# Order and width of the products in the MLPs and the attention heads of a two-layer decoder trunk

## The chip, the cores and the metric

One core of a Trainium2 chip runs the whole program. The metric is the device time of one execution in microseconds (us). TensorE (PE) multiplies; its weight loads are a row of their own in the profile (PEld). VectorE (DVE) and ScalarE (ACT) do the elementwise work, GpSimd (POOL) very little, and SyncE (SP) issues nearly all transfers.

## The reference

The input is x, 256 tokens by 1024 features, in float32. There are two layers (DEPTH = 2). The first mixes tokens with a short gated convolution, the second with attention of 8 heads in 3 groups (each group has its own window and dilation). Each mixer is followed by a squared-ReLU MLP (1024 to 4096 and back to 1024) and a gated embedding:

```python
h = h + mixed
h = h + squared_relu_mlp(rmsnorm(h, norm_mlp[i]), mlp_w_up[i], mlp_w_down[i])
ple_gate = jax.nn.sigmoid(rmsnorm(h, norm_ple[i]) @ ple_w_gate[i])
h = h + ple_gate * (p[i].astype(h.dtype) @ ple_w_proj[i])
```

In the second layer the mixer computes q, k and v for 3 x 8 heads of 128 columns from the normalised h, rotates q and k, forms softmax scores in each group, weights the values with them and projects with w_o.

## The kernel before

**Two halves of a number.** Every weight and every activation is held as a high part (`whi`, `x[0]`) and a rest (`wlo`, `x[1]`), both in fp32r. A product of the two is whi*xhi + whi*xlo + wlo*xhi. Activations are kept transposed: features on the partitions, the 256 tokens along the free axis, high part and rest side by side (`x[2]`, 2 x 256 columns).

**Blocks.** `block` (L379) issues the products of one 128 x 128 block of weights (or of 384 or 512 columns of weights). There are three kinds:
- "w": the weights are stationary. One product of 256 columns (`wlo` on xhi) and one of 512 columns (`whi` on xhi and xlo at once) go into one PSUM bank of 512 columns. The two halves of the bank are added up later by ACT and DVE (`sums`, L419). This kind does the MLPs (`up0`, `down0`, `up1`, `down1`), q and k (`qkv`), most of the convolution's input and of the output projections. I call the two products of one block a pair.
- "n": three products of 256 columns.
- "t": activations stationary, weights moving, three products of 384 columns (v) or 512 columns (the last gate).

The order of the two products of a "w" block is set at L396: the second block of two (`half` = 1) has them reversed, so that the widths run 256, 512, 512, 256, 256, 512, 512, 256 ("paired" below). An exception is made for group 0 of heads 1 to 7: there no block is reversed, and the widths run 256, 512, 256, 512 ("alternating").

**The plan.** `make_plan` (L142) is a list of blocks and steps in program order. `mlp_plan` (L66) makes an MLP: `head_start` (L51) for the first two output column pairs, then 14 more, 8 blocks of k times 2 each, with a step `up_out` behind each; a small step `stat_rows` (L499, two products of 256 columns in a bank of their own, tile ssq) falls in the middle of the up part, behind its first 128 blocks. Then 4 x 32 x 2 blocks of the down part follow.

For head h the plan (L201 to L212) runs: q and k of group 0 (16 blocks); `scores(h-1)` (L683), which also issues the products of `values(h-2)` (L729); `add_up` of group 0, which empties its two PSUM banks; groups 1 and 2 with `qk_out` (rotation) between; `turn(h-1)` (L714: transposes of the softmax, tile tp, split into pT); then the head's values v (8 rows of 128 features, 2 blocks each, 3 products of 384 columns a block) with `qk_out` and `qk_split` between, and `v_out` (L664), which empties v's two banks. Head 1 is "late": `scores(0)` comes behind group 2 and `turn(0)` behind v.

**Weights.** They come from HBM in slabs in the order in which the plan first uses them (`make_slabs`, L248), of up to 8 blocks of 128 columns (512 KB), or two rows of v (384 KB). `split_to` (L358) splits a slab into whi (ACT, L368) and wlo (DVE, L307), five slabs ahead (`LOOK`), with 5 raw and 6 split buffers. PSUM has 8 banks under one tag. Each engine's order and all waits are made from this program order by the tile framework.

Of the kernel before, what the change touches and what calls it, by code (L numbers as in the profile page):

```python
# [18 lines left out]
NK = D // P  # L19
NP = NK // 2  # L20
FF = 4 * D
HEADS = 8
# [9 lines left out]
HURRY = 250  # L32
URGENT = ("gate_out", "mix_out", "down_out", "begin")
LOOK = 5
RAW_BUFS, SPLIT_BUFS, ACT_BUFS, PAIR_BUFS = 5, 6, 13, 20


# [104 lines left out]
def make_plan():  # L142
    plan = [("do", "begin")]
# [39 lines left out]
    def qk(h, g, ks):  # L183
        return [
            ("w", "qkv", k, (i, g, h), ("qk", h, g), i, "x3") for k in ks for i in (0, 1)
        ]

    def v(h, ks):
        return [("t", "v", k, h, ("v", b, h), b, "x3") for k in ks for b in (0, 1)]
# [10 lines left out]

    for h in range(1, HEADS):  # L201

        late, scores, turn = h == 1, [("do", "scores", h - 1)], [("do", "turn", h - 1)]
        for g in range(GROUPS):
            plan += qk(h, g, range(3)) + ([("do", "qk_out", h, g - 1)] if g else []) + qk(h, g, range(3, NK))
            if g == 0:
                plan += [("do", "qk_split", 0)] if late else scores
            elif g == 2:
                plan += scores if late else turn
            plan += [("do", "add_up", ("qk", h, g))]  # L210
        plan += v(h, range(2)) + [("do", "qk_out", h, 2)] + v(h, range(2, 4)) + [("do", "qk_split", h)]
        plan += v(h, range(4, NK)) + (turn if late else []) + [("do", "v_out", h)]  # L212

    last = HEADS - 1

# [50 lines left out]
def tile_trunk(ctx: ExitStack, tc: tile.TileContext, plan, slabs, ap, out):  # L266
# [17 lines left out]
    def pair(name, tag="pair", dtype=F32R):  # L284

        if tag == "pair":
            t = apool.tile([P, 2, 2, S], dtype, tag=tag, bufs=PAIR_BUFS, name=name)
        else:
            t = cpool.tile([P, 2, 2, S], dtype, tag=tag, bufs=1, name=name)
        return t[:, :, 0, :], t[:, :, 1, :], t  # L290
# [12 lines left out]
    def flat(t):  # L303
        return t.rearrange("p i s -> p (i s)")
# [12 lines left out]
    pos = const([P, S], "pos", I32)  # L317
    h = [held("h", f"h{j}", NP + 1) for j in range(NP)]
    state = {k: {} for k in ("u", "y", "p0", "p1", "qk", "pT", *(f"x{n}" for n in range(6)))}
    acc, left, opened = {}, {}, set()  # L320
    for op in plan:
        if op[0] != "do":
            key = ((*op[4], op[5]), 0) if op[0] == "w" else (op[4], op[5] if op[0] == "n" else 0)
# [7 lines left out]
    offsets, n = [], 0  # L331
# [47 lines left out]
    def block(kind, key, k, col, name, half, operand, m=0, cuts=1):  # L379
        name = (*name, half) if kind == "w" else name  # L380
        if name not in opened:
            acc[name] = bank("acc_" + "_".join(map(str, name)))
        left[name, half if kind == "n" else 0] -= 1
        whi, wlo = weights((key, k, col))
        x = state[operand][k // 2]
        if kind == "n":
            dst = acc[name][:, half, :]
            products = ((dst, wlo, x[0][:, k % 2, :]), (dst, whi, x[1][:, k % 2, :]), (dst, whi, x[0][:, k % 2, :]))

            products = (products[2], products[0], products[1]) if key == "proj0" else products  # L390
        elif kind == "w":

            dst = acc[name]
            products = ((dst[:, 0, :], wlo, x[0][:, k % 2, :]), (flat(dst), whi, flat(x[2][:, k % 2, :, :])))

            products = products[::-1] if half and (key != "qkv" or col[1] or not col[2]) else products  # L396
        else:
            n = width(key) * P // cuts
            whi, wlo = (t[:, m * n : (m + 1) * n] for t in (whi, wlo))
            dst = flat(acc[name])[:, :n]  # L400
            xhi, xlo = (t[:, k % 2, half * P : (half + 1) * P] for t in x[:2])
            products = ((dst, xhi, whi), (dst, xhi, wlo), (dst, xlo, whi))
        for n, (to, a, b) in enumerate(products):
            nc.tensor.matmul(  # L404
                to,
                a,
                b,
                start=n == 0 and name not in opened,
                stop=n == len(products) - 1 and left[name, half if kind == "n" else 0] == 0,
                skip_group_check=True,  # L410
            )
            opened.add(name)
# [269 lines left out]

    def scores(head):  # L683

        weights = cur["pr", head] = pair(f"sm{head}", dtype=F32)[2]
        ps = [psum.tile([P, 512], F32, tag="ps", name=f"sc{head}_{b}") for b in (0, 1)]
        rest = values(head - 1) if head else None
# [26 lines left out]
    def turn(head):  # L714


        sm = cur.pop(("pr", head))
        t = cur["pT12", head] = act(f"pT12_{head}")
        nc.vector.transpose(t[:, :, :P], sm[:, :, 1, :P])
        for q, k in ((0, 1), (1, 0), (0, 2), (1, 3), (2, 0), (3, 1), (2, 3), (3, 2)):  # L720
            rows, cols = (slice(n * 32, (n + 1) * 32) for n in (q, k))
            nc.vector.transpose(t[cols, :, rows], sm[rows, :, 1, cols])
        ps = bank(f"tp{head}")
        for b in (0, 1):
            for n in (0, 1):
                nc.tensor.transpose(ps[:, n, b * P : (b + 1) * P], sm[:, b, 0, n * P : (n + 1) * P], ident)
        split_into("pT", head, ps)
# [225 lines left out]
```

## Time and profile before

| | |
|---|---|
| median of 3 runs | 771.28 us (771.0 to 771.39) |
| profiled execution, its own time | 771.19 us |
| its span in the profile | 769.4 us |
| TensorE products | 4716 |
| PE, DVE, ACT busy | 761.2, 598.6, 488.7 us |

The span is what the profile's clock covers; the execution's own time has 1.8 us more around it. A product's row in the timeline gives its start and its length; products overlap, so the distance from one start to the next, not the length, is what a product costs the engine.

### The profile page before, as it was taken

What the parts mean: (1) busy time and instruction counts of PE and PEld (TensorE: products, weight loads), DVE (VectorE), ACT (ScalarE), POOL (GpSimd) and SP (SyncE); (2) the same over time, 40 slices, a digit from 0 to 9 for tenths busy, and PEclk for the clock granted to TensorE, in tenths of its full rate; (3) what the DMA queues carried; (4) which work ended last, traced back from release to release, by engine and by line L of the source; (5) the groups of instructions that cost most, each with busy time, mean ns of one, the idle gap of its engine ahead of it and who ended that gap; (6) DMA issues with size and microseconds to landing.
All of it is one profiled execution on the core that took longest, in us unless ns stands there. A gap on an engine that the chain in (4) does not pass through costs nothing.

```text
span 769.4 us, 12415 instructions
## 1 busy us (share of the span) xinstructions
PE 761.2 (99%) x4716; PEld 680.2 (88%) x4716; DVE 598.6 (78%) x967; ACT 488.7 (64%) x796; POOL 8.9 (1%) x22
## 2 busy tenths in 40 slices
PE   9999999999999999999999999999999999999996
PEld 9988888888888899989989989989988888888885
DVE  6898789898566668898988978977899887655564
ACT  7765566666444446688887778777666555444453
POOL 0000000000000000000000000000000000000002
PEclk9999999999999999999999999999999999999999
DMA  8855555556555554554555456456465555555521
GB/s 311 312 190 192 195 191 169 190 190 197 188 190 191 192 191 139 191 187 152 169 171 197 152 162 200 147 160 219 138 192 188 193 191 191 187 188 189 184 90 56
DMA packets 42539, 140.83 MB, mean 183 GB/s; under 512 B 4848, under 2 KB 6384, under 8 KB 42480
## 3 DMA queue, kind: packets, MB, share of 16 engines
q1 hardware_dynamic: 41904, 139.39, 54.3%
q8 instruction: 37, 0.61, 0.3%
q10 hardware_dynamic: 576, 0.66, 0.3%
q14 instruction: 22, 0.18, 0.1%
HBM read 138.97 MB, written 1.05 MB: 182 GB/s over the span
## 4 chain that ended last, share of the span: by engine, by line
PE 97%; issue 1%; DMA 1%; DVE 0%; POOL 0%; SPq 0%; POOLq 0%; ACT 0%; DVEq 0%
PE acc_u L404 23%; PE acc_d L404 23%; PE acc_qk L404 18%; PE acc_v L404 9%; PE acc_o L404 6%; PE acc_g L404 5%; PE acc_B L404 3%; PE acc_C L404 3%; PE acc_X L404 3%; PE acc_p L404 1%; PE o L736 1%; PE sc L692 1%; PE o L746 1%; DMA raw<-in_w 1%; PE sc L700 1%
## 5 line engine op out<-in xcount | busy, mean ns | idle before, releaser
L307 DVE TENSOR_TENSOR wlo<-raw,whi 128x1024 fp32r<-128x1024 f32 (+2 forms) x277 | 319.2, 1155 | 126.4 <-ACT whi L368 123.9
L368 ACT ACTIVATE whi<-raw 128x1024 fp32r<-128x1024 f32 (+2 forms) x277 | 277.9, 1007 | 166.2 <-PE acc_d L404 77.1
L404 PE MATMUL acc_u<-x,whi 128*128 128x512 f32 x512 | 160.8, 396 | 0.0
L404 PE MATMUL acc_d<-u,whi 128*128 128x512 f32 x512 | 160.8, 395 | 0.0
L404 PE MATMUL acc_qk<-x,whi 128*128 128x512 f32 x384 | 124.6, 395 | 0.0
L404 PEld LDWEIGHTS acc_d<-u,wlo 128*128 128x128 f32 x512 | 96.2, 188 | 22.7
L404 PEld LDWEIGHTS acc_u<-x,wlo 128*128 128x128 f32 x512 | 96.0, 188 | 22.5
L404 PE MATMUL acc_u<-x,wlo 128*128 128x256 f32 x512 | 101.3, 278 | 0.0
L404 PE MATMUL acc_d<-u,wlo 128*128 128x256 f32 x512 | 100.9, 278 | 0.0
L404 PE MATMUL acc_qk<-x,wlo 128*128 128x256 f32 x384 | 86.9, 280 | 0.0
L404 PEld LDWEIGHTS acc_qk<-x,wlo 128*128 128x128 f32 x384 | 72.1, 188 | 12.1
L404 PEld LDWEIGHTS acc_u<-x,whi 128*128 128x128 f32 x512 | 78.0, 189 | 0.2
L404 PEld LDWEIGHTS acc_d<-u,whi 128*128 128x128 f32 x512 | 77.9, 189 | 0.0
L404 PE MATMUL acc_v<-whi,x 128*128 128x384 f32 x256 | 67.2, 337 | 0.0
L404 PEld LDWEIGHTS acc_qk<-x,whi 128*128 128x128 f32 x384 | 62.5, 188 | 4.6
L404 PEld LDWEIGHTS acc_v<-whi,x 128*128 128x128 f32 x256 | 46.5, 188 | 0.1
L404 PE MATMUL acc_v<-wlo,x 128*128 128x384 f32 x128 | 42.9, 335 | 0.0
L423 ACT ACTIVATE r<-acc_u 128x256 f32<-128x256 f32 x64 | 24.1, 378 | 27.8 <-PE acc_u L404 27.5
L404 PE MATMUL acc_o<-y,whi 128*128 128x512 f32 (+1 forms) x144 | 41.0, 370 | 0.0
L655 ACT ACTIVATE rot<-qk 16x512 f32<-16x512 f32 x48 | 30.3, 632 | 9.9 <-DVE qk L424 9.2
L424 DVE TENSOR_TENSOR r<-acc_u,r 128x256 f32<-128x256 f32 x64 | 26.5, 419 | 3.5 <-ACT r L423 3.0
L404 PEld LDWEIGHTS acc_o<-y,wlo 128*128 128x128 f32 x128 | 24.0, 188 | 5.0
(175 smaller groups left out, 976.4 us busy)
## 6 DMA issues: line engine op xcount, KB each, us to landing
raw<-in_w SPq DMA_DIRECT2D x230, 512.0 KB, 3.6
raw<-in_w SPq DMA_DIRECT2D x32, 384.0 KB, 3.4
raw<-in_w SPq DMA_DIRECT2D x10, 256.0 KB, 4.9
h<-in_xT SPq DMA_DIRECT2D x4, 256.0 KB, 5.0
gain<-in_gain SPq DMA_DIRECT2D x2, 256.0 KB, 4.6
out<-htg SPq DMA_DIRECT2D x2, 256.0 KB, 2.1
mask<-in_mask SPq DMA_DIRECT2D x2, 192.0 KB, 3.4
raw<-in_w ACTq DMA_DIRECT2D x2, 128.0 KB, 3.7
```

Source lines behind the costliest of these rows:

```text
L307: nc.vector.tensor_tensor(out, a, f32(b), ALU.subtract)
L368: nc.scalar.activation(hi[:, :width], t[:, :width], AF.Copy)
L404: nc.tensor.matmul(to, a, b, start=n == 0 and name not in opened, stop=n == len(products) - 1 and left[name, half if kind == "n" else 0] == 0,
L423: nc.scalar.activation(t[:, i, :], p[:, 1, :], AF.Copy)
L424: nc.vector.tensor_tensor(t[:, i, :], p[:, 0, :], t[:, i, :], ALU.add)
L655: nc.scalar.activation(r[dst : dst + 16], p[src : src + 16], AF.Copy)
L692: nc.tensor.matmul(ps[b][:, :S], q[:, 0, own], k[:, 1, :], start=n == 0, stop=n == 2)
L700: nc.tensor.matmul(ps[b][r * 64 : (r + 1) * 64, at : at + 64], t[:, 0, of], t[:, 1, of], start=True, stop=True)
L736: nc.tensor.matmul(ps[:, 0, :], a, b[:, kb, :], start=kb == 0 and n == 0, stop=False, skip_group_check=True)
L746: nc.tensor.matmul(ps[to, 0, q], v12[:, b, r * P + m * 64 : r * P + (m + 1) * 64], t[:, b, r * 64 : (r + 1) * 64], start=False, stop=n == ...
```

## The change

An MLP's first six "w" blocks of the up part (k = 0 and 1 of the first two column pairs, as far as `LONG_AT[:6]` goes) get a wlo product of 384 columns instead of 256: it multiplies the first 128 columns of xlo too. Their order is 384, 512. All other blocks of the up and down parts are reversed, so that the widths alternate 512, 256. Elsewhere a "w" block is reversed always where the last blocks or steps before it were of kind "t" (the set `behind` holds "long"), and otherwise only in the second half, as before; a block of kind "n", `scores` and `turn` empty the set. The exception for group 0 is gone. For heads 2 to 6 two of the eight rows of v move from behind `turn` to behind `scores`, in front of group 1. In all heads `add_up` of a group now stands in front of `scores` or `turn`, not behind.

```diff
+LONG = {"up0": (6, 384), "up1": (6, 384)}
+LONG_AT = [(k, c + i) for c in (0, 2) for k in (0, 1) for i in (0, 1)]
...
+        rows = 0 if h in (1, HEADS - 1) else 2
         late, scores, turn = h == 1, [("do", "scores", h - 1)], [("do", "turn", h - 1)]
         for g in range(GROUPS):
             plan += qk(h, g, range(3)) + ([("do", "qk_out", h, g - 1)] if g else []) + qk(h, g, range(3, NK))
+            plan += [("do", "add_up", ("qk", h, g))]
             if g == 0:
-                plan += [("do", "qk_split", 0)] if late else scores
+                plan += [("do", "qk_split", 0)] if late else scores + v(h, range(rows))
             elif g == 2:
                 plan += scores if late else turn
-            plan += [("do", "add_up", ("qk", h, g))]
-        plan += v(h, range(2)) + [("do", "qk_out", h, 2)] + v(h, range(2, 4)) + [("do", "qk_split", h)]
-        plan += v(h, range(4, NK)) + (turn if late else []) + [("do", "v_out", h)]
+        plan += v(h, range(rows, 2 + rows // 2)) + [("do", "qk_out", h, 2)] + v(h, range(2 + rows // 2, 4 + rows // 2))
+        plan += [("do", "qk_split", h)] + v(h, range(4 + rows // 2, NK)) + (turn if late else []) + [("do", "v_out", h)]
...
+        if kind != "w":
+            behind.clear()
+            behind.update(("long",) if kind == "t" else ())
...
-            products = products[::-1] if half and (key != "qkv" or col[1] or not col[2]) else products
+            first = key in LONG and (k, col) in LONG_AT[: LONG[key][0]]
+            if first:
+                n = LONG[key][1]
+                products = ((flat(dst)[:, :n], wlo, flat(x[2][:, k % 2, :, :])[:, :n]), products[1])
+            elif key[:2] in ("up", "do") or "long" in behind:
+                products = products[::-1]
+            elif half:
+                products = products[::-1]
...
     def scores(head):
+        behind.clear()
...
     def turn(head):
+        behind.clear()
```

## Rows read from the trace of the kernel before

**Rows 1.** The page: busy time of the engines, and the granted TensorE clock in 40 slices (tenths of full speed).
```profile
PE 761.2 (99%) x4716; PEld 680.2 (88%) x4716; DVE 598.6 (78%) x967; ACT 488.7 (64%) x796; POOL 8.9 (1%) x22
...
PEclk9999999999999999999999999999999999999999
```

**Rows 2.** All that TensorE's two rows waited for, by the view of waits (engine, line, for whom: us in total, times, longest).
```profile
PE warm L531 <- DVE power L527: 1.0, 1, 1.0
...
PEld acc_p L404 <- DVE wlo L307: 0.3, 1, 0.3
```

**Rows 3.** The page's costliest groups, for the counts of products (busy us, mean ns of one, idle before).
```profile
L404 PE MATMUL acc_u<-x,whi 128*128 128x512 f32 x512 | 160.8, 396 | 0.0
L404 PE MATMUL acc_d<-u,whi 128*128 128x512 f32 x512 | 160.8, 395 | 0.0
```

**Rows 4.** Stretches (us from the span's start) with their length, PE's busy time and matmul records, granted clock, DMA share and GB/s: the first half of the up part in layer 0; its down part; group 0 of heads 3 and 4; groups 1 and 2 of head 4; the values of head 4. The records in brackets count neighbours that reach into the stretch.
```profile
101.92:146.51 44.59, 44.59 (x258) 1.00 0.61 199
191.34:280.51 89.17, 89.17 (x514) 1.00 0.55 189
385.65:391.20 5.55, 5.55 (x34) 1.00 0.71 217
413.84:419.39 5.55, 5.55 (x33) 1.00 0.71 227
421.98:433.25 11.27, 11.27 (x69) 1.00 0.41 138
433.60:442.03 8.43, 8.43 (x51) 1.00 0.52 178
```

**Rows 5.** PE's timeline (start us, length us, line, tiles, count): the first gate of layer 0, 60 products of 256 columns from the first row to the last.
```profile
280.51 0.28 PE L404 MATMUL acc_g<-x,wlo 128*128 128x256 f32 x1
...
287.71 0.51 PE L486 MATMUL ssq<-ones,tot 128*128 128x2 f32 x4
```

**Rows 6.** PE's timeline at the end: nine products of 512 columns of the last gate from the first row to the last.
```profile
751.86 0.39 PE L404 MATMUL acc_g<-whi,x 128*128 128x512 f32 x1
...
753.90 0.39 PE L404 MATMUL acc_p<-whi,p 128*128 128x512 f32 x1
```

**Rows 7.** PE's timeline at the start of group 0 of head 4: the first two pairs.
```profile
413.84 0.28 PE L404 MATMUL acc_qk<-x,wlo 128*128 128x256 f32 x1
413.96 0.40 PE L404 MATMUL acc_qk<-x,whi 128*128 128x512 f32 x1
414.19 0.28 PE L404 MATMUL acc_qk<-x,wlo 128*128 128x256 f32 x1
414.31 0.39 PE L404 MATMUL acc_qk<-x,whi 128*128 128x512 f32 x1
414.54 0.27 PE L404 MATMUL acc_qk<-x,wlo 128*128 128x256 f32 x1
```

**Rows 8.** PE's timeline at group 0 of head 2, right behind `turn(0)` (tile tp): its first pairs, and the first product behind its 16 pairs.
```profile
357.35 0.36 PE L404 MATMUL acc_qk<-x,wlo 128*128 128x256 f32 x1
357.55 0.40 PE L404 MATMUL acc_qk<-x,whi 128*128 128x512 f32 x1
357.79 0.28 PE L404 MATMUL acc_qk<-x,wlo 128*128 128x256 f32 x1
357.91 0.40 PE L404 MATMUL acc_qk<-x,whi 128*128 128x512 f32 x1
358.14 0.28 PE L404 MATMUL acc_qk<-x,wlo 128*128 128x256 f32 x1
...
363.00 0.87 PE L736 MATMUL o<-pT,v 128*128 128x256 f32 x6
```

**Rows 9.** PE's timeline, head 1: its 48 products of 384 columns of v behind `scores(0)`, from the first row to the last.
```profile
348.54 0.45 PE L404 MATMUL acc_v<-whi,x 128*128 128x384 f32 x1
...
357.00 0.60 PE L726 MATMUL tp<-ident,sm 128*128 128x128 f32 x4
```

**Rows 10.** PE's timeline at the start of the MLP of layer 1, and DVE's at the same time (the rests xlo of the MLP's first operand).
```profile
553.78 0.28 PE L404 MATMUL acc_u<-x,wlo 128*128 128x256 f32 x1
553.94 0.73 PE L404 MATMUL acc_u<-x,whi 128*128 128x512 f32 x2
554.51 0.40 PE L404 MATMUL acc_u<-x,wlo 128*128 128x256 f32 x2
...
553.40 0.88 DVE L448 SCALAR_TENSOR_TENSOR x<-hr,gains,x 128x256 fp32r<-128x256 f32 x2
```

**Rows 11.** DVE's timeline during head 4's blocks, behind `scores(3)`: the values' result, the second softmax pass, the emptying of group 0's banks; behind `turn(3)`: the split of pT and of head 4's qk.
```profile
422.35 0.42 DVE L758 TENSOR_TENSOR y<-o,y 128x256 fp32r<-128x256 f32 x1
422.69 0.55 DVE L707 CUSTOM_DVE_ANT_0 sm<-sc,mask 128x384 f32<-128x384 f32 x1
423.29 0.74 DVE L424 TENSOR_TENSOR qk<-acc_qk,qk 128x256 f32<-128x256 f32 x2
...
435.62 0.68 DVE L307 TENSOR_TENSOR pT<-tp,pT 128x512 fp32r<-128x512 f32 x1
...
436.88 0.68 DVE L307 TENSOR_TENSOR qk<-qk,qk 128x512 fp32r<-128x512 f32 x1
```

**Rows 12.** ACT's timeline behind the values of head 4: the copies of v for groups 1 and 2.
```profile
443.45 2.99 ACT L676 ACTIVATE v<-acc_v,n 64x128 f32<-64x128 f32 x8
```

**Rows 13.** PE's timeline behind group 0 of head 5: the products that read pT, qk and v.
```profile
447.58 0.87 PE L736 MATMUL o<-pT,v 128*128 128x256 f32 x6
448.29 0.88 PE L692 MATMUL sc<-qk 128*128 128x256 f32 x6
449.10 0.69 PE L746 MATMUL o<-pT,v 128*64 128x64 f32 x16
```

More of the change, by code (lines that the diff above doesn't have):

```diff
@@ L319, in tile_trunk @@
     state = {k: {} for k in ("u", "y", "p0", "p1", "qk", "pT", *(f"x{n}" for n in range(6)))}
-    acc, left, opened = {}, {}, set()
+    acc, left, opened, behind = {}, {}, set(), set()
     for op in plan:
```

## The prediction

> **What bounds the kernel now.** I read the page first: PE is busy 99% of the span, PEld 88%, DVE 78%, ACT 64%, and the granted clock is in the top tenth in every slice [rows 1]; the stretches show 1.00 of full speed, the 2.4 GHz level [rows 4]. Then the waits: both TensorE rows together waited 1.3 us, all of it at the start [rows 2]. So no transfer, split or bank holds PE up, and the time is the sum over 4716 products of what each costs from its start to the next start. A change helps only if it lowers that sum, and hurts as soon as it adds columns or a wait.
>
> So I measure what a product costs in each order of widths. Uniform widths first: 60 products of 256 columns take 287.71 - 280.51 = 7.20 us, 120.0 ns each [rows 5]; nine of 512 take 753.90 - 751.86 = 2.04 us, 226.7 ns each [rows 6]. At 2.4 GHz 256 and 512 columns alone are 106.7 and 213.3 ns, so every product pays 13.3 ns on top, and a pair without loss is 346.7 ns. The MLPs run paired: the down part of layer 0 has 256 pairs (512 in both layers [rows 3]) in 89.17 us, 348.3 ns a pair, and the first 128 pairs of its up part take 44.59 us, again 348.3 [rows 4]. The alternating order stands in the trace too, in group 0: 16 pairs in 5.55 us in heads 3 and 4, 346.9 ns with the first pairs in it [rows 4]. Those first two pairs take 414.54 - 413.84 = 0.70 us [rows 7], which leaves 4.85 us for the other 14, 346.4 ns, which is 346.7 within the rows' rounding. Head 2 enters the same order from transposes and not from wide products: after its first pair it needs 363.00 - 357.79 = 5.21 us for 15 pairs, 347.3, and 346.8 without the second pair (358.14 - 357.79 = 0.35) [rows 8]. So alternating products cost 1.7 ns a pair less than paired ones.
>
> **The change part by part.**
>
> *Order in the MLPs.* There are 1024 pairs; 12 become long, 1012 go from 348.3 to 346.7: 1012 x 1.66 = 1.68 us less. From the row with its entry pairs in it (346.9) it would be 1.45 us. I take the lower price, since 500 pairs in a row are nearest to the settled ones.
>
> *The long products.* 2 x 6 blocks have 384 + 512 columns. A product of 384 costs 13.3 + 160 = 173.3 ns with the same 13.3; v's 48 take 8.43 us, 175.6 with their entry [rows 4]. A long pair is 226.7 + 173.3 = 400 ns, 51.7 over a paired one: 12 x 51.7 = 0.62 us more.
>
> *Order in the heads.* Groups 1 and 2 of heads 2 to 6 become alternating, 5 x 32 pairs x 1.66 = 0.27 us less. In head 1 the same holds for 32 pairs (no `scores` comes between), and for the first 20 pairs of w_o behind head 7's v: 0.09 less. Group 0 of head 2 stands behind `turn(0)` and goes back to paired: 0.03 more. Sum: 0.33 less.
>
> *Two rows of v behind the scores.* No product is added. What moves is the break that PE has behind the small products of `scores`. Now group 1 pays it: groups 1 and 2 of head 4 take 11.27 us, 0.12 over 32 x 348.3 ns [rows 4]. With v behind `scores`, v pays it: head 1 shows that, 357.00 - 348.54 = 8.46 us for 48 products, 0.14 over 48 x 173.3 [rows 9]. Five times 0.02 is 0.10 us more. v's break behind `turn` stays.
>
> *Start of layer 1's MLP.* The first three products, of 256, 512 and 512 columns, take 554.51 - 553.78 = 0.73 us, 0.16 over their 0.57, because the second reads xlo, whose first of two DVE pieces ends about 553.84, half of its row [rows 10]. A product of 384 columns reads xlo already, so the wait falls before the first product, with a weight load behind it: start about 554.05 in place of 553.78, 0.27 lost in place of 0.16 (an estimate from the piece's end and the 0.12 to 0.14 us that PE lost at the breaks above). I take 0.11 us more; bounds are 0.16 less (xlo earlier) and 0.3 more.
>
> *At nothing:* `add_up` in front of `scores` puts 0.74 us of DVE [rows 11] and two ACT passes ahead of the softmax; `turn` comes 11.3 us later now and 13.4 us later then. Moving a quarter of v's 8.43 us takes 2.1 us from the stretch between `turn` and the next `values`. pT is split by 436.3 and qk by 437.6, wanted at 447.58 and 448.29 [rows 11, 13]: 11 and 10 us of slack become 9 and 8. v's copies end at 446.44, wanted at 449.10 [rows 12, 13]; their distance from v's last product does not change, but up to 2.1 us more ACT work lies near it, against 2.7 us of slack. v holds two PSUM banks during groups 1 and 2; the banks of `o`, `sc` and group 0 are empty by 422.8, 423.3 and 424.0, 2.1 us at most behind the end of `scores` (421.98), and the moved v rows last 2.1 us, so group 1 finds banks. The slab of the moved rows is one of the same four of v; number and order kind stay, so SP's queue gets no more issues. If that cover fails, a head loses between nothing and the 2.1 us by which its stretch is shorter; I keep 1 us in each of 5 heads as the bound, since ACT is idle 36% of the time.
>
> **Sum:** -1.68 + 0.62 - 0.33 + 0.10 + 0.11 = -1.18 us. From the profiled execution's 771.19 that is 770.0; the median is 0.09 higher, so 770.1. About 0.2% (1.54 us) is what a measurement of this kernel can tell from no change; the forecast lies inside.
>
> **The rivals.**
>
> 1. *The order is worth nothing in the MLPs*: the 1.7 ns come from something else there than order. Then only the added columns are left: 771.28 + 0.62 + 0.10 + 0.11 = 772.1 at most. Against it: paired pairs cost 348.3 in the up part, reading x, and in the down part, reading u [rows 4]. Chance 0.11. The Trainium skill, page "TensorE: Matmul & The Clock Gate", section "Back-to-back issue gap", would have it so: it gives an isolated warm gap of N/2.4 + 2.5 ns, whatever product stands before, and by it the change would only add 12 x 128 columns, an estimate of 0.64 us from that page. The trace disagrees with it in the size, 13.3 ns and not 2.5 [rows 5, 6], and in that order matters [rows 4].
>
> 2. *Slower: the alternation settles in a worse cycle.* In the up part two products of 256 (`stat_rows`) come behind 128 blocks, in both layers; no wide product follows them, and nothing restores what the long ones set up. The entry pairs show that alternation can cost more: 0.35 us each [rows 7, 8], up to 355 ns with the rows' rounding. If it stays at 351, a little over the rows, for the 384 pairs behind that point, 768 x 2.7 = 2.1 us are added and their 1.27 us of gain are lost: 771.28 - 1.18 + 1.27 + 2.1 = 773.5. It decides from 350.2 ns a pair on (where the sum passes +1.54). Against it: head 2 left that cost after two pairs without wide products [rows 8], and no alternating stretch of the trace keeps it. Chance 0.13.
>
> 3. *A wait in the heads* takes the place of the reordering's gain: v's copies or the softmax come late by up to 1 us in five heads, giving 770.1 to 775.1, 772.6 in the middle. Slack of 2.7 us at the narrowest speaks against it [rows 12, 13]. Chance 0.08.
>
> 4. *More than forecast:* layer 1's wait vanishes, the breaks cost less: -1.68 - 0.33 + 0.62 - 0.15 = -1.54, 769.7, at the bound of what can be told. Chance 0.13.
>
> **How the numbers follow.** Forecast 0.55, and rival 1, 0.11, lie within 0.2%; so do the cheap ends of 2 and 3, 0.04 of their 0.21; 0.01 of the forecast reaches beyond 1.54. Same 0.69; slower 0.17; faster 0.13 + 0.01 = 0.14. The range takes in rivals 4 and 1 and the cheaper half of 3, and leaves out rival 2 and the rest, under 0.2: 769.5 to 772.9.
>
> **What would show it.** Right: in the profile after, the down part takes 256 x 346.7 = 88.75 us instead of 89.17, the part of the up part behind `stat_rows` 44.4 instead of 44.6, and its first part 44.7, where the long products give back the gain; groups 1 and 2 together 11.1 us behind v, without a break in front; no PE wait in the heads. Wrong: a down part of 89.2 or more, alternate pairs at 350 or more behind ssq, or PE waits on ACT at `values`.

## The result, and the profile after

The changed kernel takes 774.02 us (median of 5 runs, 773.71 to 774.38) against 771.24 for the kernel before on the same chip: ratio 1.0036, 95% interval [1.0025, 1.0048]. It is slower by 2.8 us, where the forecast was 770.1 and the range ended at 772.9. The clock is the same, so the place has to be found in stretches.

The page after, answering to [rows 1]: the same number of products, PE busy 2.3 us longer. Nothing in this view tells why.
```profile
PE 763.5 (99%) x4716; PEld 682.1 (88%) x4716; DVE 598.4 (77%) x967; ACT 484.1 (63%) x796; POOL 8.9 (1%) x22
...
PEclk9999999999999999999999999999999999999999
```

Stretches of the kernel after, as in [rows 4] (start and end, length, PE's busy time and records, clock, DMA share, GB/s): layer 0's up part before and behind its `stat_rows`, its down part; the same three of layer 1; groups 1 and 2 of head 4; from the start of w_o to the MLP of layer 1.
```profile
101.86:147.41 45.55, 45.55 (x258) 1.00 0.57 195
147.64:192.87 45.23, 45.23 (x258) 1.00 0.57 187
192.87:283.32 90.45, 90.45 (x514) 1.00 0.54 186
557.06:602.05 44.99, 44.99 (x256) 1.00 0.57 186
602.29:646.67 44.38, 44.38 (x259) 1.00 0.57 190
646.67:735.41 88.74, 88.74 (x514) 1.00 0.57 190
426.80:437.90 11.10, 11.10 (x66) 1.00 0.52 174
529.00:557.06 28.06, 27.54 (x215) 1.00 0.58 193
```
The same change of order cost 1.28 us in layer 0's down part (90.45 against 89.17) and saved 0.43 in layer 1's (88.74). In pairs: 90.45 / 256 = 353.3 ns and 88.74 / 256 = 346.7. Paired blocks took 348.3. Added up against the kernel before: layer 0's up part with `stat_rows` +1.60, its down part +1.28, layer 1's up part +0.01, its down part -0.43, the heads -0.43 (221.75 against 222.18), w_o +0.90, the start -0.06: +2.87, which is the 2.8 us of the spans (772.2 against 769.4) within rounding.

What 353.3 looks like, in PE's timeline of the kernel after in layer 0 (start, length; the distance from start to start is the price):
```profile
104.65 0.40 PE L420 MATMUL acc_u<-x,whi 128*128 128x512 f32 x1
104.89 0.28 PE L420 MATMUL acc_u<-x,wlo 128*128 128x256 f32 x1
105.01 0.40 PE L420 MATMUL acc_u<-x,whi 128*128 128x512 f32 x1
105.24 0.28 PE L420 MATMUL acc_u<-x,wlo 128*128 128x256 f32 x1
105.36 0.40 PE L420 MATMUL acc_u<-x,whi 128*128 128x512 f32 x1
105.59 0.28 PE L420 MATMUL acc_u<-x,wlo 128*128 128x256 f32 x1
105.71 0.40 PE L420 MATMUL acc_u<-x,whi 128*128 128x512 f32 x1
```
Three pairs take 105.71 - 104.65 = 1.06 us, 20 ns over three times 346.7, with no wait in any row. The trace's starts in full ns give the pairs (512, then 256) as 232/118, 241/120, 236/114, and so on without end. I call this **the costly cycle**. There are two **cheap cycles**, both of 346.7 ns a pair: an even one, every pair 230/117, and one of two pairs, 233/117 and 231/113. Group 0 of heads 3 to 7 has the two-pair cycle in the kernel before and the even one in the kernel after. In layer 1 of the kernel after the costly cycle ends without any added break, here:
```profile
568.63 0.40 PE L420 MATMUL acc_u<-x,whi 128*128 128x512 f32 x1
568.87 0.40 PE L420 MATMUL acc_u<-x,wlo 128*128 128x256 f32 x2
569.11 0.40 PE L420 MATMUL acc_u<-x,whi 128*128 128x512 f32 x1
569.35 0.28 PE L420 MATMUL acc_u<-x,wlo 128*128 128x256 f32 x1
569.47 0.39 PE L420 MATMUL acc_u<-x,whi 128*128 128x512 f32 x1
569.70 0.27 PE L420 MATMUL acc_u<-x,wlo 128*128 128x256 f32 x1
569.81 0.40 PE L420 MATMUL acc_u<-x,whi 128*128 128x512 f32 x1
```
Two products of 256 stand side by side at 568.87 (x2), as two of 512 do earlier, at 560.29, where one 512 was issued ahead of its turn; from 569.35 on a pair takes 0.34 to 0.35 us.

w_o's 0.90 us is another matter. About 0.7 of it is a wait of TensorE for pT, and 0.24 is the entry into the MLP behind it (more on both below). The view of waits, answering to [rows 2]; the 1.0 us at the start is there as before, and new is:
```profile
PEld o L754 <- DVE pT L311: 0.7, 1, 0.7
PE o L754 <- DVE pT L311: 0.4, 1, 0.4
```
DVE's timeline after, before the last head's values (wlo splits, first softmax pass, split of pT), and PE's row that waits:
```profile
537.37 2.36 DVE L311 TENSOR_TENSOR wlo<-raw,whi 128x1024 fp32r<-128x1024 f32 x2 [2.77 <-ACT whi L372]
539.64 0.55 DVE L724 CUSTOM_DVE_ANT_0 sm<-sc,mask 128x384 f32<-128x384 f32 x1
...
548.83 0.68 DVE L311 TENSOR_TENSOR pT<-tp,pT 128x512 fp32r<-128x512 f32 x1
```
```profile
549.57 0.62 PE L754 MATMUL o<-pT,v 128*128 128x256 f32 x3 [0.45 <-DVE pT L311]
```
The kernel before, at the same place, of which the prediction has no row: DVE's split of pT, and PE's first product that reads it. It ends at 546.48 and is read from 546.60, so there was 0.1 us of slack and not the 11 of head 4 [rows 11, 13].
```profile
545.80 0.68 DVE L307 TENSOR_TENSOR pT<-tp,pT 128x512 fp32r<-128x512 f32 x1
```
```profile
546.60 0.57 PE L736 MATMUL o<-pT,v 128*128 128x256 f32 x3
```

### The profile page after: what moved, and what is told of

It is laid out like the page before. It is cut to its first block, busy times and chain, and to the rows that moved or that the text cites. A ratio compares the mean times of both kernels' runs of the same rounds, so it can differ in the third digit from the quotient of the medians.

```text
span 772.2 us, 12419 instructions
## 1 busy us (share of the span) xinstructions
PE 763.5 (99%) x4716; PEld 682.1 (88%) x4716; DVE 598.4 (77%) x967; ACT 484.1 (63%) x796; POOL 8.9 (1%) x22
## 4 chain that ended last, share of the span: by engine, by line
PE 95%; DVE 1%; issue 1%; ACT 1%; DMA 1%; POOL 0%; SPq 0%; POOLq 0%; DVEq 0%
PE acc_u L420 23%; PE acc_d L420 23%; PE acc_qk L420 17%; PE acc_v L420 9%; PE acc_g L420 5%; PE acc_o L420 4%; PE acc_B L420 3%; PE acc_C L420 3%; PE acc_X L420 3%; PE acc_p L420 1%; DVE wlo L311 1%; PE o L754 1%; PE sc L709 1%; PE o L764 1%; DMA raw<-in_w 1%
## 5 line engine op out<-in xcount | busy, mean ns | idle before, releaser
L420 PE MATMUL acc_u<-x,whi 128*128 128x512 f32 x512 | 179.7, 396 | 0.0
L420 PE MATMUL acc_d<-u,whi 128*128 128x512 f32 x512 | 179.3, 396 | 0.0
L420 PE MATMUL acc_u<-x,wlo 128*128 128x256 f32 (+1 forms) x512 | 143.6, 281 | 0.1
L420 PE MATMUL acc_d<-u,wlo 128*128 128x256 f32 x512 | 142.8, 279 | 0.0
L420 PE MATMUL acc_qk<-x,whi 128*128 128x512 f32 x384 | 130.5, 392 | 0.0
L420 PEld LDWEIGHTS acc_d<-u,whi 128*128 128x128 f32 x512 | 96.1, 188 | 23.1
L420 PEld LDWEIGHTS acc_u<-x,whi 128*128 128x128 f32 x512 | 96.0, 188 | 22.9
L420 PE MATMUL acc_qk<-x,wlo 128*128 128x256 f32 x384 | 100.5, 280 | 0.0
L420 PEld LDWEIGHTS acc_qk<-x,whi 128*128 128x128 f32 x384 | 68.5, 187 | 11.4
L671 ACT ACTIVATE rot<-qk 16x512 f32<-16x512 f32 x48 | 30.3, 632 | 29.5 <-DVE qk L440 28.9
L692 ACT ACTIVATE v<-acc_v,n 64x128 f32<-64x128 f32 x64 | 23.2, 363 | 12.7 <-DVE v L688 11.9
```

The lines of the kernel that those rows point to most:

```text
L420: nc.tensor.matmul(to, a, b, start=n == 0 and name not in opened, stop=n == len(products) - 1 and left[name, half if kind == "n" else 0] == 0,
L671: nc.scalar.activation(r[dst : dst + 16], p[src : src + 16], AF.Copy)
L692: nc.scalar.activation(v12[to, b, r * P : (r + 1) * P], p[own, g * P : (g + 1) * P], AF.Copy, scale=scale[own])
```

## The experiments

Two questions: what turns the alternation costly, and what made w_o wait. The expectations give theories letters: **A**, how TensorE comes into a stretch (out of a running stream or from a break); **B**, the place (layer 0, but not layer 1); **C**, the long products; **D**, which width comes first; **P** and **F**, the place in the cycle at which the order of widths breaks; **U**, a run of one width. Layer 0 and layer 1 are L0 and L1, kernel n is that of experiment n, ssq the two products of `stat_rows`. Lengths are from PE's timeline; a half of the up part has 128 pairs, so 45.2 is the costly cycle, 44.4 a cheap one and 44.6 the paired order; for a down part 90.45, 88.75, 89.17.

**1. A break of the order in layer 0.** The changed kernel, but L0's blocks run 256 first from k = 4 on.
```diff
+            elif key in ("up0", "down0") and ("flip" in opened or (key, k, col) == ("up0", 4, 0)):
+                opened.add("flip")
             elif key[:2] in ("up", "do") or "long" in behind:
                 products = products[::-1]
```


> The changed kernel, and in layer 0 the order turns once: from the block k = 4 of the first column on, up0 and down0 run 256, 512 in place of 512, 256, so two products of 256 columns stand side by side once, as they do by chance in layer 1 at 569 us. Theory A (the order has two steady cycles, 346.7 and 353.3 ns a pair, and what stands directly before decides which one it runs in; two 256s side by side lead out of the slow one): layer 0 runs at 346.7 from there on, some 490 pairs x 6.67 ns = 3.3 us less than the changed kernel, 774.0 to 770.8. Rival B (layer 0 is slow because of what lies in layer 0: its operands, buffers, the other engines' work): it stays at 353.3, down part 90.4 us, 774.0. Rival D (256 first is the fast order, 512 first the slow one): layer 0 gets fast too, but then layer 1, 512 first and fast, is not explained.

771.59 us, ratio 1.0004 [0.9994, 1.0013]. The two 256s side by side, behind a pair 232/118, did not lead out: the half is costly. But at ssq, where three 256s stand together, L0 turned cheap: 44.37 and 88.75. So the costly cycle is no property of L0 or of its operands, and a broken order can end it, though not everywhere.

**2 and 3. Each order alone, no long products, heads as before.**
```diff
-... if half and (key != "qkv" or col[1] or not col[2]) else products
+... if half and key[:2] not in ("up", "do") and (key != "qkv" or col[1] or not col[2]) else products
```
```diff
+... if key[:2] in ("up", "do") or half and (key != "qkv" or col[1] or not col[2]) else products
```


> The kernel before, with the MLPs alone alternating, 256 first, no long products, heads as before. Layer 0 is entered from paired products that end in 256, so that two 256s stand side by side at the entry. Theory A: 346.7 ns a pair from the start in layer 0, without any long product: down part 88.75 us, 1.7 us less in both MLPs if layer 1 does the same: 769.6. Rival B: layer 0 at 353.3, down part 90.4 us: 771.3 + 2.6 - 0.9 = 773.0. Rival C (the long products are what makes the fast cycle, and were only too few): both layers at 353.3, 776.4.

> The kernel before, with the MLPs alone alternating, 512 first, no long products, heads as before. Layer 0 is entered without two 256s side by side. Theory A: layer 0 at 353.3 ns a pair (+2.6 us against paired), as with the long products, so that these do nothing; layer 1 falls to 346.7 if the scheduler again sets two 256s side by side (-0.85 us), else where its entry puts it: 773.0 or 776.4. Rival B: the same in layer 0. Rival C: both layers at 353.3, 776.4. Together with the 256-first kernel it tells A from B: the two differ in layer 0's first products alone.

256 first: 773.08, 1.0024 [1.0014, 1.0034]; L0 costly throughout (45.22, 45.23, 90.46), L1 is cheap behind its first 33 blocks (44.57, 44.38, 88.75). Those blocks hold some costly pairs too, up to 567.6 us, where two products of 512 stand side by side. 512 first: 775.74, 1.0059 [1.0043, 1.0075]; L0 costly, L1 cheap up to ssq (44.46) and costly behind it (45.23, 90.45). C falls: no long product is needed. D falls: both orders have both cycles.

**4. The heads alone**: the changed kernel with the MLPs paired.
```diff
-LONG = {"up0": (6, 384), "up1": (6, 384)}
+LONG = {}
-            elif key[:2] in ("up", "do") or "long" in behind:
+            elif key[:2] not in ("up", "do") and "long" in behind:
```


> The changed kernel's heads alone: MLPs paired as before, no long products. From the two traces: q, k and v of the heads 0.43 us less, the projection behind them 0.90 us more, since the values of the last head wait for the split of pT. Theory: 771.3 - 0.4 + 0.9 = 771.8, down parts at 89.17 us as before. Rival (the wait in the projection comes from the changed MLPs' load on DVE and ACT, not from the heads): 770.8.

771.52, 1.0004 [0.9995, 1.0014]. The MLPs are back at 89.17, the heads keep their 0.43 us gain, and w_o keeps its wait (`o` for pT, 0.5 us in the PE row; w_o takes 27.85 us against 27.17 before). The two leave +0.26 us in the span (769.65 against 769.39).

**5. Each half entered from a drained TensorE**: kernel 3 with one small float32 product in front of each up part and behind each ssq.
```diff
+    def drain():
+        keep(nc.tensor.matmul(bank("drain")[:, 0, :2], ones, ones[:, :2], start=True, stop=True))
```


> The kernel before with the MLPs alone alternating, 512 first, no long products (as the earlier kernel that had layer 0 at 353.3 ns a pair), and one added fp32 product of ones on two columns of ones, in a bank of its own that nothing reads, ahead of each up part and behind the two products of stat_rows: four in all. In the traces the fp32r product behind such a product starts 0.08 us late, with PE emptied. Theory A2 (the alternation runs at 346.7 when PE enters it emptied, and falls to 353.3 when it is entered from running paired products or thrown out of step by others): both layers at 346.7 throughout, down parts 88.75 us, 1.7 us less, four breaks of about 0.25 us more: 770.6. Rival B (layer 0 is slow for what lies in it): layer 0's down part stays at 90.4: 771.3 + 2.6 - 0.9 + 1.0 = 774.0. Rival P (pure chance of phase, no rule by entry): some of the four stretches fast, some slow.

776.38, 1.0066 [1.0054, 1.0079]. Only L1's first half is cheap (44.47); L0 on both sides of ssq (45.31, 45.31) and L1 behind ssq (45.31) are costly, though each was entered behind a break (the 512 behind it takes 323 or 324 ns to the next start instead of some 230). A falls.

**6. Long products of 512**, so that twelve products of one width open each MLP.
```diff
-LONG = {"up0": (6, 384), "up1": (6, 384)}
+LONG = {"up0": (6, 512), "up1": (6, 512)}
```


> The changed kernel with long products of 512 in place of 384 columns, so that an MLP begins with twelve products of one width, 512. Theory A2: PE is not emptied by that, layer 0 stays at 353.3 ns a pair: 774.0 + 0.6 = 774.6. Rival U (a run of one width sets the fast cycle, as the values' 384s do in the heads; the 384 beside 512 failed because they alternate themselves): layer 0 at 346.7, its down part 88.75 us: 774.6 - 3.4 = 771.2.

772.95, 1.0021 [1.0012, 1.003], neither of the two times foretold. The uniform run leads into the costly cycle in both layers (45.84 and 45.93, the added columns in them); at ssq, coming behind a pair of 232 to 233 and 118 to 119 ns, both turn to the even cheap cycle (44.38, 88.75). ssq behind 241/125, in the kernel after and in kernel 3, did not do that.

**7. Alternation everywhere**, on top of kernel 5.
```diff
-... if key[:2] in ("up", "do") or half and (key != "qkv" or col[1] or not col[2]) else products
+            products = products[::-1]
```


> As the kernel with the four added fp32 products, and every block of stationary weights in the kernel is reversed (512, 256), in the convolution, the projections and all groups of q and k too; no block or step is moved. Theory A2: groups 1 and 2 behind scores, where PE is emptied by small products, run at 346.7 without two rows of values moved there (11.20 us in place of 11.26); the convolution behind its fp32 products as well; stretches entered from running products of 256 (the projection behind the convolution, head 0) may go either way. About 500 more pairs, 0.8 us less if all are fast: 769.8; 2.5 us more if those 500 are slow: 773.1.

777.95, 1.0087 [1.0074, 1.0101], far above the 773.1 foretold as the worst: both halves of L0 and L1 behind ssq are costly as in kernel 5. Groups 1 and 2, each time behind the same small products and the same break, take 11.20 us in heads 2, 4 and 6 and 11.40 in heads 3, 5 and 7; group 0 behind v (heads 3 to 7) is cheap every time (5.55). Heads 4 and 5, stretches as in [rows 4]:
```profile
426.14:437.34 11.20, 11.20 (x68) 1.00 0.46 146
454.28:465.68 11.40, 11.40 (x68) 1.00 0.45 142
```
So a short break does not reset what decides: starts that agree within 2 ns (the first 512 takes 335 or 334) go on in the two-pair cycle in one head and in the costly one in the next.

**8. An early turn**: kernel 2, but the first two blocks of L0 have 512 first, so the order turns behind the second pair of the cycle.
```diff
+            if key[:2] in ("up", "do"):
+                products = products[::-1] if key == "up0" and (k, col) in [(0, 0), (0, 1)] else products
+            elif half and (key != "qkv" or col[1] or not col[2]):
+                products = products[::-1]
```


> The kernel before, MLPs alternating, no long products, heads as before. In layer 0 the first two blocks run 512, 256 and all later ones 256, 512, so that two 256s stand side by side once, behind the second pair; layer 1 runs 256, 512. In the earlier runs the slow cycle repeats every three pairs, with starts 232/118, 241/120, 235/114 ns apart, and two 256s led out of it behind the second of these (twice of two, layer 1) and not behind the first (once of one, layer 0). Theory F (the cycle is a matter of phase: the same products at the same point of the cycle end the same way): layer 0 runs at 346.7 ns a pair from the third block to stat_rows; what the three 256s there do depends on the phase too and is open: 346.7 behind them gives 771.3 - 0.85 - 0.67 (layer 1 as measured with 256 first) = 769.8, 353.3 gives 772.3. Rival A2 (entered from running paired products it stays slow): 353.3 throughout layer 0, 773.1.

772.13, 1.0009 [1.0, 1.0018]. PE's timeline at the turn:
```profile
102.29 0.40 PE L409 MATMUL acc_u<-x,whi 128*128 128x512 f32 x1
102.53 0.40 PE L409 MATMUL acc_u<-x,wlo 128*128 128x256 f32 x2
102.77 0.40 PE L409 MATMUL acc_u<-x,whi 128*128 128x512 f32 x1
103.00 0.28 PE L409 MATMUL acc_u<-x,wlo 128*128 128x256 f32 x1
103.12 0.39 PE L409 MATMUL acc_u<-x,whi 128*128 128x512 f32 x1
103.35 0.27 PE L409 MATMUL acc_u<-x,wlo 128*128 128x256 f32 x1
```
Behind the two 256s at 102.53 a pair takes 0.35 us, up to ssq: L0's first half 44.40, where kernel 2, without the turn, has 45.22. Theory F foretold this from the place where L1 of the kernel after left the costly cycle, also behind 241/120. Behind ssq L0 is costly again (45.23, 90.46).

**9. The sums back in their old place**: kernel 4 with `add_up` behind `scores` and `turn`.
```diff
-            plan += [("do", "add_up", ("qk", h, g))]
...
+            plan += [("do", "add_up", ("qk", h, g))]
```


> The changed kernel's heads without the moved add_up (it stands behind scores and turn again), MLPs paired as before, no long products. Theory: the 0.7 to 0.9 us that the projection behind the heads lost come from the moved add_up, which makes ACT wait for DVE in the rotation (28.9 us in the page of the changed kernel) and lets DVE split pT of the last head late; without it the values of the last head do not wait, and the heads' alternation stays: 771.3 - 0.4 = 770.9. Rival (the moved rows of v make DVE late): 771.5 as with the heads alone.

770.83, 0.9993 [0.9984, 1.0002], 0.69 us below kernel 4, the only difference being `add_up`; in the traces w_o takes 27.13 us against 27.85, and the heads are the same. DVE's timeline at the end of the heads:
```profile
531.54 2.48 DVE L311 TENSOR_TENSOR wlo<-raw,whi 128x1024 fp32r<-128x1024 f32 x2 [2.75 <-ACT whi L372]
535.43 0.56 DVE L724 CUSTOM_DVE_ANT_0 sm<-sc,mask 128x384 f32<-128x384 f32 x1 [1.41 <-PE sc L717]
...
545.17 0.68 DVE L311 TENSOR_TENSOR pT<-tp,pT 128x512 fp32r<-128x512 f32 x1
```
Here DVE waits 1.41 us for the scores before the softmax; in the kernel after the two wlo splits were only done at 539.64 and the softmax had to wait for them. PE has no wait for pT any more.

**10. A run of 384 columns in front of each half**: kernel 3 with 48 added products.
```diff
+    def run_in():
+        to = flat(bank("run_in"))[:, :384]
+        for _ in range(12):
+            keep(nc.tensor.matmul(to, ones_r, flat(state["y"][0][2][:, 0, :, :])[:, :384], start=True, stop=True))
```


> The kernel with the MLPs alternating, 512 first, no long products, and twelve added products of 384 columns (ones on a finished y, in a bank of their own that nothing reads) ahead of each up part and behind each stat_rows, 48 in all, 8.3 us. Theory U2 (a run of 384s leads into 346.7 ns a pair, as behind every row of values in the heads, 7 stretches of 7): all four stretches at 346.7, down parts 88.75 us: 771.3 - 1.7 + 8.3 = 777.9. Theory F (phase alone): no rule, some of the four at 346.7, some at 353.3, up to 783 if all are slow.

778.53, 1.0093 [1.0079, 1.0107], the added products in it. Three of four stretches are cheap (44.39; 44.37 with 88.75; 44.38 with 88.75), L1's first half costly (45.22). A run of one width is no cure either: U falls.

**11. The turn one block earlier** than in kernel 8, behind the first pair of the cycle.
```diff
-... if key == "up0" and (k, col) in [(0, 0), (0, 1)] else products
+... if key == "up0" and (k, col) in [(0, 0)] else products
```


> As the kernel that turns behind two blocks, but it turns behind one, so that the two 256s stand side by side behind the first pair (232/118) of the slow cycle. Theory F: layer 0 stays at 353.3 ns a pair to stat_rows. Rival D (one pair of 256s near the entry leads out whatever the point): 346.7. The two kernels differ in the order of two products.

770.55, 0.9988 [0.9978, 0.9997]. L0 is costly up to ssq (45.21), as F said for this place, then cheap (44.37, 88.75); L1 is cheap.

**12. Put together**: the heads of kernel 9, L1 256 first, L0 turning behind its fifth pair.
```diff
+            elif key[:2] in ("up", "do"):
+                five = [(0, 0), (0, 1), (1, 0), (1, 1), (0, 2)]
+                products = products[::-1] if key == "up0" and (k, col) in five else products
```


> What the runs point to, put together: heads as with the old place of add_up (0.45 us less), no long products, layer 1 with 256 first (0.67 us less as measured), layer 0 with 512 first for five blocks and 256 first behind them. Five is two and three: by theory F the pair of 256s again stands behind the second pair of the slow cycle's three, so layer 0 runs at 346.7 ns a pair from the sixth block on; and since the fast cycle that follows repeats every two pairs, a shift by three turns its point at stat_rows, so that the three 256s there, which led into 353.3 with two blocks, should now lead back into 346.7 (0.83 us less). Sum 771.3 - 0.45 - 0.67 - 0.83 = 769.35. Rival (the point at stat_rows does not follow from the count): layer 0 falls to 353.3 behind stat_rows, 384 x 6.67 ns = 2.6 us more: 771.9.

771.75, 1.0007 [0.9998, 1.0016]: a miss by 2.4 us. The turn did what it should (44.42 up to ssq), but ssq put L0 back into the costly cycle (45.23, 90.45). I had thought its other place in the two-pair cycle than in kernel 8 would save it. It did not.

**13 to 15. The turn behind the first, fourth and third pair**, all else as kernel 12: the costly cycle is three pairs long, so the fourth is the place of the first again.
```diff
-                five = [(0, 0), (0, 1), (1, 0), (1, 1), (0, 2)]
+                five = [(0, 0)]
```
```diff
+                five = [(0, 0), (0, 1), (1, 0), (1, 1)]
```
```diff
+                five = [(0, 0), (0, 1), (1, 0)]
```


> The heads of the changed kernel with the sums back in their old places (as in the run with the heads alone and old sums), and the MLPs of the run whose layer 0 turned behind its first pair of products. The heads lie behind layer 0's MLP, so by the theory of positions in the cycle layer 0 does what it did there: 353.3 ns a pair up to the row of ones products in the middle (45.2 us), 346.7 behind it (44.38 and 88.75), layer 1 346.7 throughout. Against the kernel before that is -0.39 in layer 0's and layer 1's up and down together as measured in that run, and -0.45 in the heads: span 768.3 to 768.4, time 770.1. Rival (the two parts disturb each other, as the run that put the phases together may suggest: the state behind the ones products is chance): 353.3 behind them in layer 0 too, +2.6, 772.6.

> The same, but layer 0 turns behind its fourth pair instead of its first. The slow cycle is three pairs long, so behind the fourth pair it stands where it stood behind the first (232/118). Theory of positions: the turn does not lead out, 353.3 up to the ones products (45.2 us), whose last product comes at the same place of the cycle as with one pair (113 and 233 ns), and 346.7 behind them; span as the run with one pair, 768.4. Rival (what matters is how many products run before the turn, or chance): fast from the turn on as behind the second and the fifth pair (44.4 us), and slow behind the ones products (45.23 and 90.45): span about 770.0.

> The same, but layer 0 turns behind its third pair, the one place of the slow cycle that no run has tried (behind a pair 235/114). The theory of positions says only that this place has one outcome of its own, not which. If the turn leads out (44.4 us to the ones products) it is into one of the two fast cycles: the one of 230/117 in every pair has come through the ones products fast each time it met them with 256 first (four times in layer 1), which would make the whole of both MLPs 346.7 and the span 767.6; the one of two pairs has turned slow there both times with 256 first, span 770.0. If it does not lead out: 45.2 us, and behind the ones products either.

13: 769.91, ratio 0.9982 [0.9973, 0.9992]. 14: one run, 769.62. 15: one run, 772.82 (before: 771.26). Stretches of 14, L0: up part before and behind ssq, down part.
```profile
101.70:146.91 45.21, 45.21 (x258) 1.00 0.62 197
147.15:191.52 44.37, 44.37 (x258) 1.00 0.58 190
191.52:280.27 88.75, 88.75 (x514) 1.00 0.58 190
```
13 has the same three lengths, 45.21, 44.37 and 88.75, and behind the turn the same starts: 256:117, 256:121, 512:237, 256:118, 512:236, 256:116, 512:224 in both. Behind the third pair the turn does not lead out (45.22), and ssq then leaves L0 costly (45.23, 90.46). L1, in all three, is in the even cycle and comes through ssq cheap.

What the runs say of an order that breaks, by the last pair before it (ns; two numbers that differ by 1 or 2 are one place):

| where | cycle and last pair | cycle behind | seen in |
|---|---|---|---|
| turn to 256 first | costly, 512:233 256:117 | costly | 1, 11, 13, 14 |
| | costly, 512:241 256:120 | cheap | 8, 12; L1 of after, 1, 7 |
| | costly, 512:236 256:113 | costly | 15 |
| ssq, 256 first | costly, 256:113 512:233 | cheap | 1, 11, 13, 14 |
| | costly, 256:117 or 118, 512:233 or 234 | costly | 2, 15 |
| | two-pair, 256:117 512:229 and 256:113 512:227 | costly | 8, 12 |
| | even, 256:117 512:229 | cheap | L1 of 2, 8, 11 to 15 |
| ssq, 512 first | costly, 512:240 256:125 | costly | after, 3 |
| | costly, 512:233 256:118 | cheap | both layers of 6 |
| | two-pair, 512:232 256:120 | cheap | L1 of after, 1 |
| | two-pair, 512:231 256:113 | costly | L1 of 3 |
| two 512s, in L1 | costly, 256:120 512:236 | costly | after, 1, 7 |
| | costly, 256:117 512:241 | cheap | 2, 8, 11 to 15 |
| | even, 256:117 512:230 | cheap | 3, 5 |
| two 256s, in L1 | even, 512:230 256:117 | cheap | 3, 5 |

The last rows, and L1's part of the second, are breaks that nobody put in: in the first blocks of L1 products are issued ahead of their turn, and the order is made up for 30 to 50 products later. There L1 leaves the costly cycle in ten of the kernels. No place of the table has had two outcomes. It holds for breaks of the order inside a running stream; behind a wait or a break of TensorE, as in kernel 7, starts alike within 2 ns have led both ways.

## Why the prediction was wrong

**The step that failed: "Order in the MLPs"**, -1.68 us. It took 346.7 ns a pair from group 0 of the heads [rows 4, 7, 8] and carried it to 1012 pairs elsewhere. That is the price of the cheap cycles, and group 0 behind v's 384s is in one of them each time (heads 3 to 7, in the kernel before, the kernel after and kernel 7); experiment 10 shows that a run of 384s does not always lead there. In L0 alternation entered behind the paired blocks of the convolution's output projection is costly, in every kernel without added products in front: 506 pairs x (353.3 - 348.3) = 2.53 us more. L1 behind ssq got the forecast price, 384 x 1.66 = 0.64 us less. Sixteen pairs per head, entered in other ways, could not show a second cycle that runs on for 500. One sum in that working is off: head 2 without its second pair is (5.21 - 0.35) / 14 = 347.1 ns and not 346.8, which changes nothing here.

**Rival 2** was right in kind and in sign: alternation settles in a worse cycle, and by more than the point of 350.2 from which it decides. It had the place wrong (behind `stat_rows` in both layers; in fact from L0's entry, and not in L1) and the size (351; 353.3). Its 773.5 is near 774.02 partly by chance, since the wait below is in the latter. Its argument against itself, that head 2 left the cost after two pairs, came from the heads again. **Rival 1** fell: order matters, in both directions. The Trainium skill, page "TensorE: Matmul & The Clock Gate", section "Back-to-back issue gap", gives a gap that depends on the width alone. The rows of this case do not bear it out: they have three prices for the same two widths, 346.7, 348.3 and 353.3 ns a pair.

**The long products:** forecast +0.62, measured about 0.70. 122 x 353.3 ns + 6 long pairs = 45.55 us in L0 leaves 407 ns for a long pair, and the starts there give 231 + 175 = 406: 6 to 7 over the forecast 400. The mechanism was right, and kernels 2 and 3 show that the costly cycle comes without them.

**Heads and rows of v:** right in kind and sign, too small in size. Groups 1 and 2 of head 4 take 11.10 us as said, 0.17 less than before, and its values take 2.19 + 6.33 = 8.52 us (424.61 to 426.80 and 438.24 to 444.57) against 8.43. So the moved break costs 0.09 us where I took 0.14, and a head gains 0.08 us, five heads 0.4. Forecast -0.23 with the breaks, measured -0.43 in all.

**"At nothing":** wrong for `add_up`. The cover that I named, 8 to 11 us of slack for pT and qk, was read at head 4. At the last head the slack is 0.1 us, and I had no row of it. Price 0.7 us by kernels 4 and 9 (771.52 against 770.83); the rest of w_o's 0.90 is the entry into L1's MLP, below. This is rival 3's kind of wait, but on DVE and at one place, not in five heads. How `add_up` moves DVE's two wlo splits in front of the softmax is seen in the timelines: ACT copies v late because DVE's part of v comes late, and ACT's whi and DVE's wlo stand behind that copy. In kernel 9 the same copy starts without a wait, at 527.43. That the lateness begins with ACT's waits for DVE before the rotation was not tried by itself; these waits are 28.9 us in all in the kernels after and 4, 16.8 in kernel 9 and 9.2 in the kernel before. ACT's timeline at the copy of v, and the page's group of the rotation, both of the kernel after:
```profile
533.24 3.00 ACT L692 ACTIVATE v<-acc_v,n 64x128 f32<-64x128 f32 x8 [1.75 <-DVE v L688]
...
L671 ACT ACTIVATE rot<-qk 16x512 f32<-16x512 f32 x48 | 30.3, 632 | 29.5 <-DVE qk L440 28.9
```

**Start of layer 1:** forecast +0.11, 0.27 us lost in place of 0.16. The rows of the kernel after:
```profile
556.59 0.40 PE L420 MATMUL acc_o<-y,whi 128*128 128x256 f32 x2
557.06 0.41 PE L420 MATMUL acc_u<-x,wlo 128*128 128x384 f32 x1
557.31 0.40 PE L420 MATMUL acc_u<-x,whi 128*128 128x512 f32 x1
```
The last two products of w_o have 0.47 us where two of 256 need 0.24, and the first long product takes 0.25 instead of 0.175: about 0.31 lost, 0.15 more than before, within the bounds given. Of that 0.24 stands in front of the MLP and so counts with w_o above. L1's up part as a whole is +0.01: its first half, 44.99, holds some 26 costly pairs ((568.87 - 559.58) / 0.353, from the long pairs' end to the change) beside the long ones.

**What stays open.** That the place in the cycle decides how a break of the order ends is shown: 13 and 14 agree to the ns with 6 products between their turns, 15 between them goes another way, and no place of the table has two outcomes. The starts do not show all of what decides, as kernel 7 says. What in the engine keeps count, why the costly cycle is three pairs long, and why two-pair and even cycles differ at ssq, no run here shows. The table is a record of these widths and operands, not a rule. A layer 0 that is cheap throughout was not found; it would save another 0.84 us (45.21 to 44.37).

**A better version** came of it: kernel 13, 769.91 us against 771.26, 0.9982 of the kernel before, and 4.1 us below the changed one. It keeps the heads' order, drops the long products and the moved sums, runs 256 first, and turns L0 behind its first pair:
```profile
102.04:147.25 45.21, 45.21 (x258) 1.00 0.64 197
147.49:191.86 44.37, 44.37 (x258) 1.00 0.59 190
191.86:280.61 88.75, 88.75 (x513) 1.00 0.58 190
553.41:597.97 44.56, 44.56 (x259) 1.00 0.58 188
598.20:642.58 44.38, 44.38 (x258) 1.00 0.58 189
642.58:731.33 88.75, 88.75 (x514) 1.00 0.57 190
```
Against [rows 4] the down parts gain 0.42 us each; L0's first half, 45.21, is what is left.

## What to carry to other kernels

A price per product read from a short stretch holds for that stretch's neighbours: before carrying it to hundreds of products, look for the period of the starts, and ask whether the new place is entered in the same way. Where such cycles exist, sum the starts of each half after a change; one total hides a gain and a loss. And slack has to be read at every place where a moved step acts, the last head above all, not at a typical one.

## What was not expected of the hardware

With no wait in the trace and the full clock, the same products in the same order cost 346.7 or 353.3 ns a pair for as long as the stretch lasts, and one product out of order can switch between them. A break of some 0.1 us, as behind the scores, does not reset it: in kernel 7 the same groups behind the same break alternate between 11.20 and 11.40 us from head to head.
